# Quarter passes for the third column group of the experts, with a branch at its transposes

## The chip, the cores and the metric

The kernel runs on one core of a Trainium2 chip. A run's time is device microseconds from start to end; three runs of the kernel before took 1610.56, 1611.50 and 1614.88 us, a median of 1611.5. One more execution was profiled; its own time was 1617.83 us.

## The reference

The program is two layers of a transformer block on 256 tokens of width 1024. The second layer ends in a mixture of experts, and only that part is touched here:

```python
probs = jax.nn.softmax(logits, axis=-1)
top_p, top_i = lax.top_k(probs, TOP_K)              # 2 of 8 experts for a token
...
for e in range(N_EXPERTS):
    out = out + combine[..., e:e + 1] * _swiglu(h, w1[e], w3[e], w2[e])
# _swiglu: (silu(h @ w1) * (h @ w3)) @ w2, with w1, w3 of 1024 x 2816 and w2 of 2816 x 1024, fp32
```

The kernel gives each expert only the tokens that chose it. How many these are depends on the data: 64 on average, up to 128 in the part of the program that matters here (more than 128 would start a second pass, which these inputs don't need).

## The kernel before

**Weights.** The weights of an expert come as 35 blocks, each one DMA of 256 rows (two k-tiles of 128): 24 for W1 and W3 and 11 for W2. The 2816 inner columns are cut in three groups, two of 1024 columns and one of 768. For a group, four blocks of W1 follow each other and then four of W3 (`for g in range(3)`, L1665 on); after the groups come the 11 blocks of W2 with 1024 columns each. A block is 1 MB, or 768 KB in the third group. All DMAs are issued by SyncE (L97) in this order into 16 buffers, each as soon as a buffer is given back by the block that last used it.

**Tokens as the stationary operand.** In `passes` (L1613) the tokens of an expert are the weights of TensorE's array and the expert's weights stream through. For the first 64 tokens ("kind 0") the array is used as two halves of 64 columns: two matmuls side by side, one for the lower and one for the upper half of the group's inner columns, so that a bank of PSUM holds tokens by inner columns twice (`tiles`, L1615 to L1619). What happens for tokens beyond 64 is decided at run time by the count `num[e]` (`more`, L1597):

- up to 64 tokens: nothing more;
- up to 96: in the first two groups and in W2 the remaining 32 tokens ("kind 2") take four matmuls of 32 columns side by side, each over a quarter of the block's columns (`quart`, m = 32); in the third group they take the path of the next line;
- over 96: 64 more tokens ("kind 1") in two halves, like the first ones, into the second bank (`half`).

Branches are real ones: TensorE's sequencer compares and jumps (L1602 for 64, L1606 for 96). The other engines run the same instructions on either path.

**Between W3 and W2.** ScalarE takes silu of the W1 banks (L1687), VectorE multiplies by the W3 banks (L1689), and `transposes` (L1643) turns the product into W2's stationary operand: TensorE transposes of 128 columns (L1650), four for a group of 1024 and three for the third, for each of the two banks, and a copy to SBUF. `hidden` (L1656) finds the 64 or 32 tokens that belong to a k-tile in it. In the third group a quarter layout had no counterpart there, since 768 columns in quarters are 192, one and a half tiles; so `quarters` was passed as `g < 2`.

**Order.** A scheduler puts the instructions of every engine in a fixed order; an If with its bodies stays in one piece. In the first expert blocks of the next expert's W1 stand between the late W2 blocks. An expert's number in this text is its place in the order of work: the first is expert 0 of the model, the fourth the one with the most tokens.

Of the kernel before, what the change touches and what calls it, by code (L numbers as in the profile page):

```python
# [8 lines left out]
F32 = mybir.dt.float32  # L9
# [17 lines left out]
CAP = 128  # L27
# [155 lines left out]
HALF = 64  # L183
QUART = 32
# [25 lines left out]
def _body(ctx, tc, nc, I, out):  # L210
    V, A, PE, G, SP = nc.vector, nc.scalar, nc.tensor, nc.gpsimd, nc.sync
# [10 lines left out]
    def ps_x():  # L222
        return psx.tile([128, 512], F32, name="px", tag="px")
# [7 lines left out]
    def ctile(shape, dt=F32, name=None, pool=None):  # L231
        cnt[0] += 1
        name = f"{name}{cnt[0]}"
        return (mconst if pool else const).tile(shape, dt, name=name, tag=name)
# [11 lines left out]
    ident = ctile([128, 128], name="ident")  # L246
# [297 lines left out]
    cur = {}  # L544
# [854 lines left out]
    def moe_route():  # L1399

        Sp, M = pools["s"], pools["m"]
# [65 lines left out]
        def places(out, src):  # L1467
            for b in range(2):
                V.tensor_tensor(out=tmp[:, b], in0=src[:, b].unsqueeze(1).to_broadcast(sq), in1=ord_, op=OP.mult)
            V.tensor_reduce(out=out, in_=tmp, axis=AX.X, op=OP.add)  # L1470
# [4 lines left out]
        quart = M.tile([128, NE], F32, name="qu", tag="qu")  # L1475

        def tail():

            V.tensor_copy(out=fl[:, 2], in_=pos[:, 16:16 + NE])
            V.tensor_copy(out=fl[:, 3], in_=iota[:, 0:NE])  # L1480
            places(rt[:, 0:1, 12:14].rearrange("p o a e -> p (o a) e"), fl[:, 2:4])
            V.tensor_copy(out=cm[:, 1:].rearrange("p (a e) -> p a e", a=2), in_=rt[0:1, 0, 12:14])
            V.tensor_reduce(out=fl[:, 0, 0:1], in_=fl[:, 2], axis=AX.X, op=OP.max)
            V.tensor_copy(out=cm[:, 0:1], in_=fl[0:1, 0, 0:1])
            V.tensor_scalar(out=quart, in0=rt[:, 0, 12], scalar1=float(HALF + QUART), scalar2=None, op0=OP.is_le)
            V.tensor_tensor(out=rt[:, :, 3, 2:3], in0=rt[:, :, 4, 0:1], in1=rt[:, :, 4, 1:2], op=OP.add)
            V.reciprocal(out=rt[:, :, 3, 3:4], in_=rt[:, :, 3, 2:3])
            V.tensor_tensor(out=rt[:, :, 6, 0:2], in0=rt[:, :, 4, 0:2],
                            in1=rt[:, :, 3, 3:4].to_broadcast([128, 2, 2]), op=OP.mult)
            for i in range(2):  # L1490
                V.tensor_tensor(out=t(7 + i), in0=t(7 + i), in1=col(6, i), op=OP.mult)
            V.tensor_tensor(out=t(14), in0=t(7), in1=t(8), op=OP.add)
            places(t(10), t(14))

        cur["moe"] = dict(r=r, rt=rt, cm=cm, key=key, quart=quart, tail=tail)

    def moe_pass(stream, off, raw_pool, finish):
# [6 lines left out]
        M = lambda: pools["m"]  # L1504
# [3 lines left out]
        def block(W, j, c0, n, k0):  # L1508

            def src():  # L1510
                if j == 0:
                    w = W[0:1]
                else:
                    if j not in ids:
                        ids[j] = nc.values_load(cur["moe"]["cm"][0:1, 1 + NE + j:2 + NE + j],
                                                engines=[mybir.EngineType.SP], min_val=0, max_val=NE - 1)
                    w = W[bass.ds(ids[j], 1)]
                return w[:, k0 * 128:k0 * 128 + 256, c0:c0 + n].rearrange("o (k p) c -> p (o k) c", p=128)
            return stream.raw(src, 2, n, raw_pool)
# [5 lines left out]
        hp = []  # L1525
# [67 lines left out]
        def run_pend():  # L1593
            while pend:
                pend.pop(0)()

        def more(e, half, quart, none=lambda: None):  # L1597

            if off:
                half()  # L1600
                return
            with tc.If(num[e] > HALF) as c:  # L1602
                if quart is None:
                    half()
                else:
                    with tc.If(num[e] > HALF + QUART) as c2:  # L1606
                        half()
                    with c2.Else():
                        quart()
            with c.Else():  # L1610
                none()

        def passes(e, banks, w, n, lhs, first, last, quarters):  # L1613

            def tiles(bank, kind, k, m):  # L1615
                c = n // (128 // m)
                for q in range(128 // m):
                    PE.matmul(out=bank[m * q:m * q + m, 0:c], lhsT=lhs(kind, k), rhs=w[:, k, c * q:c * q + c],  # L1618
                              start=first and k == 0, stop=last and k == 1)  # L1619

            def rest():
                tiles(banks[0], 0, 1, HALF)

            def half():
                for k in range(2):
                    tiles(banks[1], 1, k, HALF)
                rest()

            def quart():
                for k in range(2):  # L1630
                    tiles(banks[1], 2, k, QUART)
                rest()

            tiles(banks[0], 0, 0, HALF)
            more(e, half, quart if quarters else None, rest)

        def expert(e):
            gt = {}
            gT = {}
            y = []  # L1640
            tabs = {}

            def transposes(g):  # L1643
                nb = 4 if g < 2 else 3
                gT[g] = M().tile([128, 2, nb, CAP], F32, name="gt", tag="gt" if g < 2 else "gt2")
                for i in range(2):
                    p = ps_x()
                    pv = p.rearrange("p (c s) -> p c s", c=4)[:, 0:nb]
                    for c in range(nb):
                        PE.transpose(out=pv[:, c], in_=gt[g][:, i, c * 128:c * 128 + 128], identity=ident)  # L1650
                    if i == 0:
                        A.activation(out=gT[g][:, i], in_=pv, func=AF.Copy)  # L1652
                    else:
                        V.tensor_copy(out=gT[g][:, i], in_=pv)

            def hidden(kk, kind):  # L1656

                g, d = min(kk // 8, 2), kk - 8 * min(kk // 8, 2)
                nb = 4 if g < 2 else 3
                if kind == 2 and g < 2:  # L1660
                    return gT[g][:, 1, d % 2, QUART * (d // 2):QUART * (d // 2) + QUART]
                c = HALF * (d // nb)
                return gT[g][:, min(kind, 1), d % nb, c:c + (HALF if kind < 2 else QUART)]

            for g in range(3):  # L1665
                n = 1024 if g < 2 else 768
                for wi, W in enumerate((W1, W3)):
                    for i in range(4):
                        raw = block(W, e, g * 1024, n, 2 * i)

                        def fn(hi, lo, g=g, n=n, wi=wi, i=i):
                            def lhs(kind, k):
                                c = (0, HALF, HALF)[kind]
                                return xg[e][:, 2 * i + k, c:c + (HALF, HALF, QUART)[kind]]

                            passes(e, hp[wi], hi[0], n, lhs, i == 0, i == 3, g < 2)
                            if wi == 0 and i == 1:
                                run_pend()
                                if g > 0:
                                    transposes(g - 1)  # L1680
                            if i == 3:
                                if wi == 0:
                                    gt[g] = M().tile([128, 2, 512], F32, name="esg", tag="s")
                                for b in range(2):
                                    c = slice(0, n // 2)
                                    if wi == 0:
                                        A.activation(out=gt[g][:, b, c], in_=hp[0][b][:, c], func=AF.Silu)  # L1687
                                    else:
                                        V.tensor_tensor(out=gt[g][:, b, c], in0=gt[g][:, b, c], in1=hp[1][b][:, c],  # L1689
                                                        op=OP.mult)  # L1690
                        stream.unit([sub(raw, lambda t: t, "raw")], fn)
            for ch in range(11):
                raw = block(W2, e, 0, 1024, ch * 2)

                def fn(hi, lo, ch=ch):
                    if ch == 0:
                        y.extend((ps_x(), hp[1][1]))
                    passes(e, y, hi[0], 1024, lambda kind, k: hidden(2 * ch + k, kind), ch == 0, ch == 10, True)
                    if ch == 1:
                        tabs["t"] = scatter_table(e)  # L1700
                    if ch == 2:
# [130 lines left out]
    start = res[0]  # L1832
# [32 lines left out]
    n = nc.values_load(cur["moe"]["cm"][0:1, 0:1], min_val=0, max_val=T)  # L1865
    with tc.If(n > CAP):
        rest = Stream(nc, wpool, WB)
        rest.open(["a"], [rawa], 2048, [RA])
        start = moe_pass(rest, CAP, "a", moe_finish)
# [27 lines left out]
```

## Time and profile before

| | |
|---|---|
| three runs | 1610.56, 1611.50, 1614.88 us (median 1611.5) |
| profiled execution | 1617.83 us, span 1616.1 us |
| PE (matmuls) busy | 1530.3 us, 95% of the span |
| DVE, ACT, POOL busy | 771.8, 577.9, 46.3 us |
| read from HBM | 455.58 MB, 283 GB/s over the span |
| weight blocks of the experts | 216 issues of 1024 KB and 64 of 768 KB |
| expert stage | from some 905 us to the end |
[...]

How to read it: PE and the DMA engines both look full over the expert stage, and the shares of the whole span say nothing of which of them ends last at a given place. The stage has to be cut into stretches. An fp32 matmul shows as two records of PE (and two weight loads, PEld), so record counts are twice the matmuls. The ends of matmul records are modelled and overlap the next ones; paces are read from the starts, as a stretch divided by the blocks in it.

### The profile page before, as it was taken

Reading aid. Unit: us, or ns where it says so; the run is one execution under the profiler, and the core shown is the slowest. Engines: PE = TensorE matmul, PEld = TensorE weight load, DVE = VectorE, ACT = ScalarE, POOL = GpSimd, SP = SyncE. Lnnn points to the kernel's source line nnn. Section 1 sums busy time; section 2 is a strip of 40 time slices with the busy share of each in tenths; the row PEclk is TensorE's granted clock in tenths of the full one; section 3 lists DMA queues with packets and bytes.
Section 4 is the critical chain, followed back from the end, with each engine's and each line's share of the span. In section 5 each row is a group of like instructions: output and inputs, shape, how many; then the busy total and the mean of one; then the engine's idle time right before and its main releaser. Section 6 shows DMA issues by size and latency. Waiting matters only on the chain. (4 is left out here: it accounts for less than half of the span.)

```text
span 1616.1 us, 26236 instructions
## 1 busy us (share of the span) xinstructions
PE 1530.3 (95%) x10586; PEld 1071.7 (66%) x10586; DVE 771.8 (48%) x1274; ACT 577.9 (36%) x924; POOL 46.3 (3%) x68
## 2 busy tenths in 40 slices
PE   3999999999989999999999899999899999999996
PEld 2999899989988999999999333343334333333332
DVE  7899687776776659976575310111101111110121
ACT  3676656655444477775764100011000010100010
POOL 2001010000000000002000000000000000000000
PEclk9999999999999999999998899999999999999998
DMA  9656677435688743554448599999999899999995
GB/s 363 234 184 205 242 249 282 161 127 193 240 280 310 263 149 117 184 196 157 157 157 331 185 351 334 393 407 404 408 405 397 277 380 407 404 407 405 408 404 212
DMA packets 162780, 459.29 MB, mean 284 GB/s; under 512 B 11454, under 2 KB 19716, under 8 KB 162600
## 3 DMA queue, kind: packets, MB, share of 16 engines
q1 hardware_dynamic: 162408, 456.55, 76.5%
q8 instruction: 140, 2.29, 0.6%
q14 instruction: 40, 0.33, 0.1%
q0 software_dynamic: 192, 0.11, 0.0%
HBM read 455.58 MB, written 1.05 MB: 283 GB/s over the span
## 5 line engine op out<-in xcount | busy, mean ns | idle before, releaser
L1618 PE MATMUL pm<-rawa,xg 128*64 128x512 f32 (+2 forms) x2368 | 412.8, 519 | 6.6 <-DMA rawa<-in_moe_w 2.9
L122 DVE TENSOR_TENSOR wl<-rawa,wh 128x1024 fp32r<-128x1024 f32 (+1 forms) x243 | 293.8, 1215 | 99.5 <-ACT wh L120 98.5
L120 ACT ACTIVATE wh<-rawa 128x1024 fp32r<-128x1024 f32 (+1 forms) x243 | 254.8, 1054 | 230.4 <-PE pm L578 107.7
L1618 PEld LDWEIGHTS pm<-rawa,xg 128*64 128x64 f32 (+1 forms) x2368 | 141.7, 130 | 259.7 <-issue 241.6
L577 PE MATMUL pm<-hh,wh 128*128 128x256 f32 x992 | 286.5, 289 | 5.6 <-ACT hh L552 4.6
L579 PE MATMUL pm<-hh,wl 128*128 128x256 f32 x992 | 284.2, 287 | 4.0 <-DVE wl L122 4.0
L578 PE MATMUL pm<-hl,wh 128*128 128x256 f32 x992 | 284.6, 287 | 1.6 <-DVE hl L553 0.8
L577 PEld LDWEIGHTS pm<-hh,wh 128*128 128x128 f32 x992 | 190.1, 192 | 9.1 <-ACT hh L552 4.8
L579 PEld LDWEIGHTS pm<-hh,wl 128*128 128x128 f32 x992 | 189.8, 191 | 5.3 <-DVE wl L122 5.0
L578 PEld LDWEIGHTS pm<-hl,wh 128*128 128x128 f32 x992 | 189.8, 191 | 2.9 <-DVE hl L558 1.2
L1618 PE MATMUL px<-rawa,gt 128*64 128x512 f32 x704 | 167.0, 599 | 5.6 <-DMA rawa<-in_moe_w 4.9
L1689 DVE TENSOR_TENSOR esg<-esg,pm 128x512 f32<-128x512 f32 (+1 forms) x48 | 29.5, 641 | 281.5 <-PE pm L1618 281.2
L591 PE MATMUL pm<-wl,hh 128*128 128x256 f32 x448 | 128.7, 287 | 1.6 <-DVE wl L122 1.6
L590 PE MATMUL pm<-wh,hh 128*128 128x256 f32 x448 | 128.8, 288 | 0.0
L592 PE MATMUL pm<-wh,hl 128*128 128x256 f32 x448 | 127.8, 285 | 0.0
L1618 PEld LDWEIGHTS px<-rawa,gt 128*64 128x64 f32 x704 | 46.9, 136 | 98.3 <-issue 88.9
L414 DVE SCALAR_TENSOR_TENSOR macc<-rawm,csil,macc 128x1024 f32<-128x1024 f32 x74 | 94.6, 1278 | 35.0 <-DMA rawm<-in_w_mod 34.6
L591 PEld LDWEIGHTS pm<-wl,hh 128*128 128x128 f32 x448 | 84.9, 189 | 2.0 <-DVE wl L122 1.8
L592 PEld LDWEIGHTS pm<-wh,hl 128*128 128x128 f32 x448 | 84.9, 189 | 0.2 <-issue 0.2
L590 PEld LDWEIGHTS pm<-wh,hh 128*128 128x128 f32 x448 | 84.9, 190 | 0.0
L1716 DVE COPY ys<-pm 128x512 f32<-128x512 f32 x8 | 5.5, 692 | 161.4 <-PE pm L1618 83.9
L1652 ACT ACTIVATE gt<-px 128x512 f32<-128x512 f32 (+1 forms) x24 | 13.5, 564 | 181.6 <-PE px L1650 181.6
(401 smaller groups left out, 1960.7 us busy)
## 6 DMA issues: line engine op xcount, KB each, us to landing
rawa<-in_moe_w SPq DMA_DIRECT2D x216, 1024.0 KB, 17.6
rawa<-in_w_in SPq DMA_DIRECT2D x68, 1024.0 KB, 6.2
rawa<-in_moe_w SPq DMA_DIRECT2D x64, 768.0 KB, 15.0
rawm<-in_w_mod SPq DMA_DIRECT2D x80, 512.0 KB, 8.3
rawa<-in_ffn_w SPq DMA_DIRECT2D x29, 1024.0 KB, 7.4
rawa<-in_w_branch SPq DMA_DIRECT2D x12, 1024.0 KB, 5.7
rawa<-in_w_out SPq DMA_DIRECT2D x8, 1024.0 KB, 5.5
rawa<-in_w_mod SPq DMA_DIRECT2D x7, 1024.0 KB, 10.1
```

The lines of the kernel that those rows point to most:

```text
L120: nc.scalar.activation(out=hv, in_=src, func=AF.Copy)
L122: nc.vector.tensor_sub(out=lv, in0=src, in1=hv.bitcast(F32))
L414: V.scalar_tensor_tensor(out=st["acc"], in0=src[:, 0], scalar=csil[:, k:k + 1], in1=st["acc"], op0=OP.mult, op1=OP.add)
L577: PE.matmul(out=o, lhsT=wh, rhs=xh[:, k], start=(k == 0), stop=False)
L578: PE.matmul(out=o, lhsT=wh, rhs=xl[:, k], start=False, stop=False)
L579: PE.matmul(out=o, lhsT=wl, rhs=xh[:, k], start=False, stop=(k == nk - 1))
L590: PE.matmul(out=o, lhsT=xh[:, k, c], rhs=wh, start=(k == 0), stop=False)
L591: PE.matmul(out=o, lhsT=xh[:, k, c], rhs=wl, start=False, stop=False)
L592: PE.matmul(out=o, lhsT=xl[:, k, c], rhs=wh, start=False, stop=(k == nk - 1))
L1618: PE.matmul(out=bank[m * q:m * q + m, 0:c], lhsT=lhs(kind, k), rhs=w[:, k, c * q:c * q + c], start=first and k == 0, stop=last and k == 1)
L1652: A.activation(out=gT[g][:, i], in_=pv, func=AF.Copy)
L1689: V.tensor_tensor(out=gt[g][:, b, c], in0=gt[g][:, b, c], in1=hp[1][b][:, c], op=OP.mult)
```

## The change

The third group gets the quarter path too: for 65 to 96 tokens the 32 tokens beyond 64 take four matmuls of 32 columns over 192 inner columns each, and the product is transposed in another layout: two transposes of 128 columns at offsets 0 and 64, and two matmuls of 64 columns that put columns 128 to 191 and 0 to 63 into the third tile, the second by way of `turn`, an identity rotated by 32 that POOL copies once. This layout is chosen by a branch at the transposes of the third group's second bank. In every block the second k-tile of the first 64 tokens now stands ahead of the matmuls for the tokens beyond 64 instead of behind them (the parameter `odd` is always False).

```diff
@@ moe_route, tail
+            turn = M.tile([128, CAP], F32, name="turn", tag="otmp")
+            G.tensor_copy(out=turn[:, 0:CAP - QUART], in_=ident[:, QUART:CAP])
+            G.tensor_copy(out=turn[:, CAP - QUART:CAP], in_=ident[:, 0:QUART])
+            cur["moe"]["turn"] = turn
@@ passes
-            def rest():
-                tiles(banks[0], 0, 1, HALF)
+            def rest(ks):
+                for k in ks:
+                    tiles(banks[0], 0, k, HALF)
             def half():
                 for k in range(2):
                     tiles(banks[1], 1, k, HALF)
-                rest()
             def quart():
                 for k in range(2):
                     tiles(banks[1], 2, k, QUART)
-                rest()
-            tiles(banks[0], 0, 0, HALF)
-            more(e, half, quart if quarters else None, rest)
...
+                rest((0,))
+                more(e, lambda: (rest((1,)), half()), lambda: (rest((1,)), quart()), lambda: rest((1,)))
@@ transposes
+                    def odd():
+                        for c in range(2):
+                            PE.transpose(out=pv[:, c], in_=src[:, c * 64:c * 64 + 128], identity=ident)
+                        PE.matmul(out=pv[0:64, 2], lhsT=src[:, 128:192], rhs=ident, start=True, stop=True)
+                        PE.matmul(out=pv[64:128, 2], lhsT=src[:, 0:64], rhs=cur["moe"]["turn"], start=True, stop=True)
+                    if i == 1 and g == 2 and not off:
+                        more(e, blocks, odd, blocks)
+                    else:
+                        blocks()
@@ hidden
-                if kind == 2 and g < 2:
-                    return gT[g][:, 1, d % 2, QUART * (d // 2):QUART * (d // 2) + QUART]
...
+                c, q = (d % 2, d // 2) if g < 2 else ((0, 0), (2, 0), (1, 1), (0, 2), (2, 2), (1, 3))[d]
+                return gT[g][:, 1, c, QUART * q:QUART * q + QUART]
@@ expert
-                            passes(e, hp[wi], hi[0], n, lhs, i == 0, i == 3, g < 2)
+                            passes(e, hp[wi], hi[0], n, lhs, i == 0, i == 3, False)
```

The order of PE's instructions in a block of the third group, here the first one of the first expert. `64x384` is a matmul of 64 columns with 384 streamed columns, `x2` two of them; all bodies of a branch are listed, the one for over 96 tokens first. Before (L1618 matmuls, L1602 the comparison with 64):

```order
L1618 MATMUL pm<-rawa,xg 64x384 x2
L1602 COMPARE_AND_BRANCH
L1618 MATMUL pm<-rawa,xg 64x384 x6
L1602 UNCONDITIONAL_BRANCH
L1618 MATMUL pm<-rawa,xg 64x384 x2
L1602 UNCONDITIONAL_BRANCH
```

After (L1623 matmuls, L1606 the comparison with 64, L1610 the one with 96):

```order
L1623 MATMUL pm<-rawa,xg 64x384 x2
L1606 COMPARE_AND_BRANCH
L1610 COMPARE_AND_BRANCH
L1623 MATMUL pm<-rawa,xg 64x384 x6
L1610 UNCONDITIONAL_BRANCH
L1623 MATMUL pm<-rawa,xg 64x384 x2
L1623 MATMUL pm<-rawa,xg 32x192 x8
L1610 UNCONDITIONAL_BRANCH
L1623 MATMUL pm<-rawa,xg 64x384 x2
L1606 UNCONDITIONAL_BRANCH
```

A body of eight matmuls of 32 columns and 192 streamed columns has come in, behind the two that finish the first 64 tokens, and a second comparison. With up to 64 tokens the same four matmuls run as before.

PE's order around the first W2 block of the first expert (`gt` is W2's stationary operand, `esg` the product that the transposes read; L1650, then L1660 and L1665 to L1667, are the transposes). Before:

```order
L1602 COMPARE_AND_BRANCH
L1606 COMPARE_AND_BRANCH
L1618 MATMUL pm<-rawa,gt 64x512 x4
L1618 MATMUL px<-rawa,gt 64x512 x2
L1606 UNCONDITIONAL_BRANCH
L1618 MATMUL pm<-rawa,gt 32x256 x8
L1618 MATMUL px<-rawa,gt 64x512 x2
L1606 UNCONDITIONAL_BRANCH
L1618 MATMUL px<-rawa,gt 64x512 x2
L1602 UNCONDITIONAL_BRANCH
L1650 MATMUL px<-ident_83,esg 128x128 x6
```

After, without the bodies of the W2 block's branch:

```order
L1660 MATMUL px<-ident_83,esg 128x128 x3
L1606 COMPARE_AND_BRANCH
...
L1606 COMPARE_AND_BRANCH
L1610 COMPARE_AND_BRANCH
L1660 MATMUL px<-ident_83,esg 128x128 x3
L1610 UNCONDITIONAL_BRANCH
L1665 MATMUL px<-ident_83,esg 128x128 x2
L1666 MATMUL px<-ident_83,esg 64x128
L1667 MATMUL px<-turn,esg 64x128
L1610 UNCONDITIONAL_BRANCH
L1660 MATMUL px<-ident_83,esg 128x128 x3
L1606 UNCONDITIONAL_BRANCH
```

The three transposes of the first bank have moved ahead of the W2 block's branch; those of the second bank stay behind it and are now the three bodies of a branch of their own.

## Rows read from the trace of the kernel before

**Rows 1.** Busy time of each engine in stretches of the expert stage (heading first).

```profile
core 0: us, PE busy (x) PEld busy (x) DVE busy (x) ACT busy (x) POOL busy (x), PEclk, DMA share, GB/s
954.30:979.00 24.70, 24.70 (x148) 10.71 (x144) 4.25 (x12) 2.45 (x5) 0.00 (x0) 1.00 0.96 340
979.00:1018.00 39.00, 38.92 (x301) 12.87 (x302) 1.56 (x4) 0.49 (x1) 0.00 (x0) 1.00 0.93 345
1018.00:1140.00 122.00, 120.36 (x602) 47.82 (x600) 24.80 (x52) 14.33 (x28) 0.00 (x0) 1.00 1.02 402
1140.00:1160.00 20.00, 16.24 (x72) 4.46 (x70) 0.69 (x1) 0.60 (x1) 0.00 (x0) 1.00 1.02 408
1160.00:1245.00 85.00, 84.56 (x432) 33.47 (x434) 10.60 (x21) 5.82 (x11) 0.00 (x0) 1.00 1.03 407
1245.00:1300.00 55.00, 55.00 (x250) 20.65 (x248) 6.62 (x13) 3.94 (x7) 0.00 (x0) 1.00 0.84 287
1300.00:1385.00 85.00, 83.08 (x406) 29.25 (x402) 14.16 (x27) 7.77 (x15) 0.00 (x0) 1.00 1.02 403
1385.00:1400.00 15.00, 11.49 (x66) 4.31 (x64) 1.76 (x4) 1.47 (x3) 0.00 (x0) 1.00 1.03 403
1400.00:1590.00 190.00, 188.81 (x1228) 70.85 (x1230) 29.65 (x54) 16.03 (x31) 0.00 (x0) 1.00 1.03 406
```

**Rows 2.** What the SyncE queue waited for, 954 to 1018 us: us, times, longest.

```profile
SPq L97 <- PE px L1618: 26.4, 11, 4.0
SPq L97 <- PE pm L1618: 18.5, 8, 2.9
```

**Rows 3.** Timeline at the last weight block: start, us, what, idle before.

```profile
1599.41 1.94 PE L1618 MATMUL px<-rawa,gt 128*64 128x512 f32 x8 [0.57 <-DMA rawa<-in_moe_w]
```

**Rows 4.** Groups by shape on PE, 880 us to end: count, busy, mean ns.

```profile
L1618 PE MATMUL pm<-rawa,xg 128*64 128x384 f32 x704 | 120.6, 489 | 2.3 <-DMA rawa<-in_moe_w 2.3
L1618 PE MATMUL pm<-rawa,xg 128*32 128x256 f32 x512 | 34.3, 385 | 0.0
```

**Rows 5.** Groups by shape, 915 to 1016 us (first expert).

```profile
L1618 PE MATMUL pm<-rawa,xg 128*64 128x384 f32 x128 | 22.5, 490 | 0.0
L1618 PE MATMUL pm<-rawa,xg 128*32 128x256 f32 x208 | 13.9, 385 | 0.0
L1650 PE MATMUL px<-ident,esg 128*128 128x128 f32 x22 | 3.3, 283 | 0.0
L1689 DVE TENSOR_TENSOR esg<-esg,pm 128x384 f32<-128x384 f32 x2 | 1.1, 555 | 6.2 <-PE pm L1618 6.1
```

**Rows 6.** Groups by shape on PE, 1430 to 1534 us (seventh expert).

```profile
L1618 PE MATMUL pm<-rawa,xg 128*64 128x384 f32 x128 | 21.3, 488 | 0.0
L1618 PE MATMUL pm<-rawa,xg 128*32 128x256 f32 x256 | 17.1, 385 | 0.0
```

**Rows 7.** Stretches of whole blocks, columns as in rows 1.

```profile
935.22:946.68 11.46, 11.46 (x98) 3.61 (x96) 0.00 (x0) 0.00 (x0) 0.00 (x0) 1.00 0.93 335
971.05:978.83 7.78, 7.78 (x49) 3.36 (x48) 1.52 (x5) 1.85 (x4) 0.00 (x0) 1.00 0.96 325
1171.73:1185.44 13.71, 13.71 (x66) 5.52 (x64) 0.54 (x1) 0.60 (x1) 0.00 (x0) 1.00 1.02 407
```

**Rows 8.** Timeline of the weight loads of one quarter block's narrow passes.

```profile
935.22 0.59 PEld L1618 LDWEIGHTS pm<-rawa,xg 128*32 128x32 f32 x16 [0.81 <-issue]
```

**Rows 9.** Page, section 3: instruction DMAs, packets, MB, share.

```profile
q8 instruction: 140, 2.29, 0.6%
```

**Rows 10.** The first comparison's line: ns min/median/max, first and last start.

```profile
L1602 PEldq COMPARE_BRANCH  x312: 65/208/4868, 902.9 to 1602.1; - x156
```

**Rows 11.** Waits from 880 us on: us, times, longest.

```profile
PE pm L1618 <- issue: 2.8, 6, 1.0
```

More of the change, by code (lines that the diff above doesn't have):

```diff
@@ L1611, in more, with passes @@
                 none()
-        def passes(e, banks, w, n, lhs, first, last, quarters):
+        def passes(e, banks, w, n, lhs, first, last, odd):
             def tiles(bank, kind, k, m):
@@ L1631, in quart @@
                     tiles(banks[1], 2, k, QUART)
-                rest()
-            tiles(banks[0], 0, 0, HALF)
-            more(e, half, quart if quarters else None, rest)
+            if odd:
+                more(e, lambda: (half(), rest((0, 1))), lambda: (quart(), rest((0, 1))), lambda: rest((0, 1)))
+            else:
+                rest((0,))
+                more(e, lambda: (rest((1,)), half()), lambda: (rest((1,)), quart()), lambda: rest((1,)))
         def expert(e):
@@ L1648, in transposes, with blocks @@
                     pv = p.rearrange("p (c s) -> p c s", c=4)[:, 0:nb]
-                    for c in range(nb):
-                        PE.transpose(out=pv[:, c], in_=gt[g][:, i, c * 128:c * 128 + 128], identity=ident)
+                    src = gt[g][:, i]
+                    def blocks():
+                        for c in range(nb):
+                            PE.transpose(out=pv[:, c], in_=src[:, c * 128:c * 128 + 128], identity=ident)
+                    def odd():
[5 more added lines that the diff above has]
+                        more(e, blocks, odd, blocks)
+                    else:
+                        blocks()
                     if i == 0:
@@ L1659, in hidden @@
                 nb = 4 if g < 2 else 3
-                if kind == 2 and g < 2:
-                    return gT[g][:, 1, d % 2, QUART * (d // 2):QUART * (d // 2) + QUART]
-                c = HALF * (d // nb)
-                return gT[g][:, min(kind, 1), d % nb, c:c + (HALF if kind < 2 else QUART)]
+                if kind < 2:
+                    c = HALF * (d // nb)
+                    return gT[g][:, kind, d % nb, c:c + HALF]
+                c, q = (d % 2, d // 2) if g < 2 else ((0, 0), (2, 0), (1, 1), (0, 2), (2, 2), (1, 3))[d]
+                return gT[g][:, 1, c, QUART * q:QUART * q + QUART]
             for g in range(3):
@@ L1697, in fn @@
                         y.extend((ps_x(), hp[1][1]))
-                    passes(e, y, hi[0], 1024, lambda kind, k: hidden(2 * ch + k, kind), ch == 0, ch == 10, True)
+                    passes(e, y, hi[0], 1024, lambda kind, k: hidden(2 * ch + k, kind), ch == 0, ch == 10, False)
                     if ch == 1:
```

## The prediction

> **What bounds the kernel now.** I read the expert stage alone (905 to 1616 us), since the change touches nothing ahead of it but two copies. First the busy time by stretch, for who has no room: PE or the DMA engines. The reader is to see two limits that take turns [rows 1]. The most that the DMA engines move is about 408 GB/s, and PE is busy nearly throughout, so neither alone tells which of them ends last. In the first expert (its third group and W2, 954 to 1018) PE has next to no idle time and the DMA engines move 340 to 345 GB/s. There the SyncE queue, which issues the weight loads, spends 44.9 of the 64 us from 954 to 1018 waiting for PE to give a buffer back [rows 2]: PE is the limit, and it hands its pace on to the DMA engines. From 1018 to 1140 they run at 402, and at 1140 to 1160 PE is idle 3.8 us (20.00 less 16.24): the limit has become the DMA. From 1245 to 1300, in the large fourth expert, PE has no idle time and the DMA engines fall to 287 GB/s: PE again. From 1300 to 1590 it is 403 to 406 GB/s, PE is idle 3.5 us at 1385 to 1400, and the last block's matmuls begin after a gap of 0.57 us that ends with the landing of their weights [rows 3]: DMA to the end.
>
> Then the shapes, for which experts the edit reaches. Each fp32 matmul leaves two records. A block of the third group gives 8 records of 64 columns x 384 for the first 64 tokens and 8 more for the second half; 8 experts of 8 blocks make 512, and the 704 there leave 192, three experts with over 64 tokens [rows 4]. The 32-wide form has 512 records in the first two groups, 256 an expert: two experts take the quarter path. One is the first expert and the other the seventh, at 1430 to 1534 [rows 5, 6]. The fourth takes the half path and runs the same matmuls as before.
>
> **The change part by part.** *A block of the third group.* Three stretches give the paces at full clock [rows 7]. Fourth expert: 13.71 us hold four half blocks (64 records and two tails), 3.43 each, which is 8 passes (two matmuls of 64 columns side by side) of 0.43 us for 512 columns. First expert, third group: 7.78 us hold three half blocks, 2.59 each, 8 passes of 0.324 for 384 columns. So a pass goes by its columns. Quarter block of the first groups: 11.46 us hold four, 2.87 each. Its four wide passes take 1.72 and its four narrow ones (four matmuls of 32 columns side by side, 256 long) half of that, 0.86, by columns: 2.58. The other 0.29 is what two changes of width cost, 64 to 32 and back. The third group has none of them now, since it uses 64 columns alone; the change brings two to every block. A new block: four wide passes of 0.324 make 1.29, four narrow ones of 192 columns 0.65 at 0.162, two changes 0.29: 2.23 us. Against 2.59 that is 0.36 a block, 2.9 us in an expert.
>
> The unmeasured term is the 192-column pass. By columns it is 0.162; if something in the narrow form sets its pace it stays at the 0.216 of 256 columns, the block is 2.44 and the expert saves 1.2 us. It can't beat its columns, unless the change of width shrinks as well; with that at nothing an expert saves 5.2. I take 0.162: 16 narrow weight loads start within 0.59 us [rows 8], 37 ns each, and a pass has four, 0.148.
>
> [...]
>
> *Order inside a block.* The second k of the first 64 tokens now stands before the narrow passes, inside the branch. The number of width changes stays at two. Bank 0 is ready earlier, bank 1 later; at the end of the third group the first transposes stand before the branch of the first W2 block and wait for VectorE's product on bank 0, which now runs beside the narrow passes. Nothing, while they cover it; if they don't, one product of 384 columns, 0.56 us (1.1 for two), once an expert [rows 5].
>
> *The transposes.* Three become two wide ones and two of 64 columns side by side. 22 records take 3.3 us [rows 5], 0.30 a transpose, so the matmuls cost between 0 and 0.30 more, and there are two more changes of width, 0.29. I take 0.3 in the first expert. The other experts run the same three behind two more jumps.
>
> *The two copies on POOL.* POOL is at 0.00 in every stretch [rows 1] and PE needs them 70 us later: nothing.
>
> *More instructions.* PE's program grows from 9021 to 9331 rows, 3.4%. Of 2.29 MB of instructions for all engines [rows 9] that is at most 0.08 MB, 0.2 us at 408 GB/s.
>
> *Where the two gains go.* First expert: 2.9 − 0.3 = 2.6 us on PE. Its buffers come back sooner, one each 2.23 us, while a 1 MB load takes 2.57 at 408 GB/s; so 8 x 0.34 = 2.7 us of loads are put off into 979 to 1018, where the engines have 39.0 x (1 − 345/408) = 6.0 us to spare. From there all moves up by 2.6: the DMA-bound stretch, the PE-bound fourth expert, the DMA-bound rest. Seventh expert: it stands in the last DMA-bound stretch. PE comes earlier to the last weights, and waits. In the profile that leaves nothing. The profiled execution took 1617.8 (a span of 1616.1 and 1.7 around it) and the median run 1611.5, 6.3 less; if a part of this is faster loads, PE and DMA end closer together than the 0.57 us shows, and some of the gain survives. I put it between 0 and 2.6 and take 0.6.
>
> Sum: −2.6 − 0.6 + 0.2 = −3.0 us, 1617.8 to 1614.8 in a profile, and on the median 1608.5.
>
> **The rivals.** *Both experts pay.* If outside the profile the tail is bound by PE, the second 2.6 counts: −5.2 + 0.2, 1606.5; with cheaper changes of width some 1605. For it: the 6.3 us between profile and runs, and PE at 188.8 of 190 us busy before 1590. Against it: the gap of 0.57 that ends with a DMA, and 3.5 us of idle PE just ahead of the seventh expert.
>
> *The narrow pass keeps its pace.* 1.2 − 0.3 in the first expert, with 0.2 for code: 1610.8, no change. For it: the shorter the pass, the more any fixed part weighs, and 0.148 of loads stand close to 0.162.
>
> *Slower: jumps get exposed.* In the PE-bound first and fourth expert all 16 third-group blocks now hold a second compare and longer bodies to jump over. A compare has a median of 208 ns, and PE lost 2.8 us in 6 gaps without a releaser, 0.47 each [rows 10, 11]. One such gap a block makes 7.5 us: −3.0 + 7.5, 1616.0, and with any in the transposes or the DMA-bound experts beyond. It decides from 0.19 us a block on. Against it: the quarter blocks of the first two groups carry the same compares and jumps, and their 2.87 is all accounted for above; the fourth expert's blocks carry them too and run at 3.43, 8 passes of 0.43.
>
> [...]
>
> **How the numbers follow.** First expert alone, with a part of the seventh: 0.46. Both: 0.22. No shorter pass: 0.18. Jumps: 0.11. Anything else: 0.03. A measurement of this kernel tells 0.3%, 4.8 us, from no change, so faster begins at 1606.7. Nearly all of "both" and a little of the likeliest lie there: 0.24. Slower needs 1616.3: about 0.11. Within: 0.65. The range goes from "both" with cheaper changes of width, 1604, to the pace kept plus what runs differ by upward (1614.9 against 1611.5), 1613.5.
>
> **What would show it.** In the profile after, the 64 x 384 form has 576 records and a 32 x 192 form 256. The third group of the first expert takes 2.9 us less than its 24.7, with narrow passes 0.162 apart; passes 0.216 apart show the second rival, gaps ahead of the first matmul behind a jump the third. The DMA engines reach 400 GB/s about 2.6 us earlier, before 1018, and PE waits some 3 us for the last weights in place of 0.57. If that wait has not grown while PE has less to do, the seventh expert pays as well and my reading of the tail is wrong. If the first expert's third group is shorter and the stretch at 1140 to 1160 begins no earlier, the hand-over from PE to DMA is wrong.

## The result and the profile after

The changed kernel took 1626.15 us (median of six runs, 1621.58 to 1626.76) and the kernel before, on the same chip, 1612.37 (six runs, 1609.61 to 1617.81). The ratio is 1.0081, its 95% interval 1.0063 to 1.0098: slower by 0.8%, 13.8 us between the medians. The prediction was 1608.5, with 1604.0 to 1613.5 as its range. Its sign is wrong.

The narrow passes came as predicted. Three blocks of the first expert's third group after, columns as in [rows 1] (to be read against the second line of [rows 7]):

```profile
968.27:974.96 6.69, 6.69 (x73) 2.71 (x72) 1.17 (x4) 1.74 (x4) 0.00 (x0) 1.00 0.97 328
```

6.69 us for three are 2.23 a block, the predicted figure, against 2.59 in [rows 7]. The shapes of the seventh expert after, 1435 to 1537 us, columns as in [rows 6]:

```profile
L1623 PE MATMUL pm<-rawa,xg 128*64 128x384 f32 x64 | 12.1, 499 | 0.0
L1623 PE MATMUL pm<-rawa,xg 128*32 128x192 f32 x128 | 6.9, 332 | 0.0
```

Half of the 384-column records are gone and 128 narrow ones are there, in this expert and in the first. So the time was lost elsewhere. In the changed kernel TensorE's products stand at line 1623 and its transposes at 1660 to 1667. The waits of TensorE in the expert stage after, 895 to 1620 us (us in total, times, longest):

```profile
PE pm L1623 <- issue: 18.1, 17, 2.0
PE px L1748 <- ACT ys L1738: 1.4, 2, 0.7
PE px L1623 <- issue: 1.2, 1, 1.2
...
PE px L1660 <- DVE esg L1712: 0.7, 1, 0.7
```

And in the kernel before, the lines beside [rows 11]:

```profile
PE px L1618 <- DMA rawa<-in_moe_w: 4.9, 6, 1.8
PE pm L1618 <- DMA rawa<-in_moe_w: 2.9, 5, 0.9
```

"Issue" is time in which nothing that the profile shows held the engine back. It went from 2.8 us in 6 gaps [rows 11] to 18.1 in 17 (3.6 of it in two gaps of the first expert that have another cause, below), while the 7.8 us of waits for weights vanished: TensorE is now so late that every weight block is there before it is wanted. The stretches after show the same, columns as in [rows 1]:

```profile
954.30:979.00 24.70, 23.95 (x237) 10.18 (x235) 4.37 (x12) 2.83 (x6) 0.00 (x0) 1.00 0.99 358
979.00:1018.00 39.00, 38.28 (x282) 12.18 (x278) 1.25 (x2) 1.57 (x3) 0.00 (x0) 1.00 0.91 327
1018.00:1140.00 122.00, 114.73 (x555) 46.00 (x555) 21.99 (x42) 11.49 (x22) 0.00 (x0) 1.00 1.03 405
...
1400.00:1590.00 190.00, 182.36 (x1272) 67.39 (x1270) 29.72 (x54) 14.54 (x28) 0.00 (x0) 1.00 1.03 406
```

From 1018 to 1140 TensorE is now idle 7.3 us (1.6 in [rows 1]) and from 1400 to 1590 7.6 us (1.2). Where, a timeline of PE in the third expert (at most 64 tokens, a *plain* one from here on) tells: start, us, what, and in brackets the idle time before.

```profile
1113.53 5.37 PE L1623 MATMUL pm<-rawa,xg 128*64 128x512 f32 x24 [0.85 <-issue]
1119.39 4.09 PE L1623 MATMUL pm<-rawa,xg 128*64 128x512 f32 x20 [0.48 <-issue]
...
1125.24 0.87 PE L1623 MATMUL pm<-rawa,xg 128*64 128x384 f32 x4 [0.60 <-issue]
...
1131.00 4.09 PE L1623 MATMUL pm<-rawa,xg 128*64 128x384 f32 x24 [0.72 <-issue]
1136.76 0.87 PE L1623 MATMUL pm<-rawa,xg 128*64 128x384 f32 x4 [1.67 <-issue]
```

The gaps stand 5.76 to 5.86 us apart, whatever the shape. From 1131.00 to 1136.76 three blocks are run (24 records, 8 a block); they need 4.09 us, and then the engine stands for 1.67. The DMA queues tell what comes at that pace. Section 3 of the profile after (against [rows 9]):

```profile
q8 instruction: 152, 2.49, 0.6%
```

And the same queue in the 34 us from 1108 to 1142 alone:

```profile
q8 instruction: 6, 0.10, 1.2%
```

I take a packet of this queue for a piece of the program, an *instruction page* (a page from here on): 2.49 MB / 152 = 16.4 KB. Six in 34 us are one every 5.7 us. Three of the packets start at 1122.72, 1128.47 and 1134.22 us, and the gaps above end 2.5 us after each, at 1125.24, 1131.00 and 1136.76. So, as I read it, the engine gets a page, runs three blocks from it, and waits for the next.

### The profile page after: what moved, and what is told of

It is laid out like the page before. It is cut to its first block, busy times and chain, and to the rows that moved or that the text cites. A ratio compares the mean times of both kernels' runs of the same rounds, so it can differ in the third digit from the quotient of the medians.

```text
span 1624.0 us, 26544 instructions
## 1 busy us (share of the span) xinstructions
PE 1534.5 (94%) x10720; PEld 1078.2 (66%) x10720; DVE 772.0 (48%) x1274; ACT 577.9 (36%) x924; POOL 47.7 (3%) x70
## 3 DMA queue, kind: packets, MB, share of 16 engines
q8 instruction: 152, 2.49, 0.6%
## 5 line engine op out<-in xcount | busy, mean ns | idle before, releaser
L1623 PE MATMUL pm<-rawa,xg 128*64 128x512 f32 (+3 forms) x2496 | 409.2, 503 | 18.7 <-issue 18.1
L1623 PEld LDWEIGHTS pm<-rawa,xg 128*64 128x64 f32 (+1 forms) x2496 | 140.1, 128 | 271.2 <-issue 256.8
L1623 PE MATMUL px<-rawa,gt 128*64 128x512 f32 x704 | 167.2, 598 | 1.2 <-issue 1.2
L1623 PEld LDWEIGHTS px<-rawa,gt 128*64 128x64 f32 x704 | 50.1, 136 | 88.4 <-issue 84.1
L1710 ACT ACTIVATE esg<-pm 128x512 f32<-128x512 f32 (+1 forms) x48 | 24.3, 559 | 155.5 <-PE pm L1623 155.5
```

## What the experiments were to tell apart

Three theories. *Code*: the third group now writes out 20 products a block in the program (2 ahead of the branch, 6, 10 and 2 in its bodies) where it had 10 (2, 6, 2), a product being one matmul of the program, two records in the trace; a plain expert runs 4 of them in 1.3 us, but the pages hold all, and they arrive no faster. *Jumps*: it is the compares and jumps, not what is jumped over. *Order*: it is the second pair of products that now stands ahead of the passes for the tokens beyond 64.

**The third group's bodies alone, never run.** The kernel before, with a body of quarter passes in the third group behind a count that doesn't occur (where `off` is set it stays as before):

```diff
-            more(e, half, quart if quarters else None, rest)
+            if quarters or off:
+                more(e, half, quart, rest)
+            else:
+                with tc.If(num[e] > HALF) as c:
+                    with tc.If(num[e] > 250) as c2:
+                        quart()
+                    with c2.Else():
+                        half()
+                with c.Else():
+                    rest()
```

> The kernel before, with a body in each third-group block that is never entered: for over 64 tokens a second comparison, with 250, chooses between a quarter body (eight matmuls of 32x192 and the two of the first 64 tokens) and the half body that before ran alone. No count reaches 250, so what runs is what ran before, plus one comparison a block in the three experts over 64 tokens; 640 matmuls more lie in PE's program. Code theory (the bodies that are jumped over are fetched with the rest, a 16 KB page takes some 5.8 us while the weight loads fill the DMA engines, and experts of up to 64 tokens run through a page sooner): slower than before by 10 to 17 us, gaps without a releaser ahead of the third group's matmuls in the plain experts, 9 to 12 more instruction packets. Jump theory (each comparison and jump in the PE-bound experts is exposed): also slower, 8 to 15 us, but with gaps in the first and fourth expert. Order theory (the loss comes from the new order inside a block and at the transposes): no change.

Measured: 1618.37 us, ratio 1.0040 (1.0018 to 1.0061), 7 us slower without one product more to run. Its waits of PE, 895 to 1620 us:

```profile
PE pm L1618 <- issue: 13.7, 15, 1.8
PE px L1618 <- issue: 2.6, 4, 1.6
```

Its program has 151 pages (2.47 MB) where the kernel before has 140 [rows 9], and but for the first expert's the gaps stand in the plain experts, as in the changed kernel. TensorE's products in the expert stage come in exactly the order of the kernel before. The loss is below the range that I gave the code theory (10 to 17 us), so code can't be all of the 13.8.

**The same compare and jumps with a short body.** As above, with `rest()` in place of `quart()`: 12 products a block.

> The same with a short body that is never entered: only the two matmuls of the first 64 tokens. The comparisons and jumps are those of x1_dead, the code grows by 128 matmuls in place of 640. Code theory: a fifth of the loss of x1_dead, 0 to 4 us slower than before. Jump theory: the same loss as x1_dead within 3 us. Order theory: no change.

Measured: 1614.76 us, 1.0021 (1.0008 to 1.0034), 143 pages. Its largest wait for issue, 895 to 1620 us:

```profile
PE pm L1618 <- issue: 2.0, 4, 1.0
```

The order of TensorE's products is again that of the kernel before, and as many compares and jumps run as in the run above. The jump theory wanted that run's time within 3 us; it is 3.6 us faster, with intervals that overlap, so it is the gaps that decide, and they are there only with the longer body. The 512 products between the two programs are 8 pages, 64 to a page. The 3.5 us by which this run still is slower than the kernel before I can't place: none of its traced waits has grown by more than 0.2 us, and its expert stage, from the start of the first product to the start of the last, is no longer than that of the kernel before (694.5 us against 695.6; 702.1 in the run above).

**The order alone.** The kernel before with `rest()` ahead of the passes in `half` and `quart`, nothing else.

> The kernel before with the new order inside a block alone: the second k-tile of the first 64 tokens stands at the head of the branch's bodies, the matmuls for the tokens beyond 64 behind it. Third group on the half path, transposes and amount of code as before. Order theory: slower by 8 to 14 us. Code and jump theory: slower by 1 to 4 us, from the loads of the counts in the first expert, whose two gaps grew from 0.58 and 1.03 us to 1.58 and 2.05, and from the wait for VectorE at the first transposes.

Measured: 1617.28 us, 1.0039 (1.0021 to 1.0057). More than the code theory allowed, less than the order theory wanted. Its first two waits for issue are in the first expert, 895 to 925 us, where PE loads the counts (three and four register loads between blocks). The same two waits there in this run, in the changed kernel, and in the kernel before:

```profile
PE pm L1618 <- issue: 3.6, 2, 2.0
```
```profile
PE pm L1623 <- issue: 3.6, 2, 2.0
```
```profile
PE pm L1618 <- issue: 1.6, 2, 1.0
```

The loads begin while the last products ahead of them are still in the array. In the old order the last ones are a pair of 512 columns, and in the kernel before the first loads start 1.7 and 1.8 us ahead of the end of these products; in the new order they are narrow passes, and in the changed kernel it is 0.7 and 0.8 us. So the cover is a microsecond shorter, twice. With the wait of the first transposes for VectorE (0.7) and one more for ScalarE's `ys` (0.7), which these two kernels share, the order costs 3.4 us that can be pointed at; the expert stage is 3.3 us longer than in the kernel before (698.9 against 695.6). The rest of the 6.1 us between the medians is not placed.

**Four products ahead of the branch, an empty body.** The changed kernel with both pairs first:

```diff
-                rest((0,))
-                more(e, lambda: (rest((1,)), half()), lambda: (rest((1,)), quart()), lambda: rest((1,)))
+                rest((0, 1))
+                more(e, half, quart)
```

> The changed kernel with shorter code: both k-tiles of the first 64 tokens stand once ahead of the branch, and its bodies hold only the matmuls for the tokens beyond 64 (none for up to 64). What runs is the same, in the same order. PE's program has 424 matmuls less than before, 1120 less than the changed kernel. Code theory: the gaps without a releaser in the plain experts go, the first and seventh experts keep their third group of some 22 and 19 us: 3 to 10 us faster than before, some 1605. Jump theory: as slow as the changed kernel, 1622 to 1628, since the jumps are the same. Order theory: 1622 to 1628 as well, since the order is the same.

Measured: 1676.17 us, 1.0396 (1.0371 to 1.0421). A miss by 70 us, by something that I had not thought of. All gaps for issue went; others came. Its waits, 895 to 1680 us:

```profile
PE pm L1623 <- PEq L1606: 11.3, 48, 0.8
PE px L1660 <- DVE esg L1712: 6.0, 7, 0.9
PE px L1623 <- PEq L1606: 5.4, 27, 0.4
```

PEq is the sequencer. One of its records on the line of the branch, columns as in [rows 10]:

```profile
L1606 PEldq EVENT_SEMAPHORE  x180: 51/51/51, 1006.2 to 1664.7; - x180
```

The changed kernel has 5 of these on the same line; with a body without a product in every block there are 180. In the records the instruction starts some 40 ns behind the modelled end of the last product, so the array drains 180 times. The plain blocks take 2.09 us in place of 1.72; 180 x 0.37 is 67 us, an estimate, against 65 us above the kernel before.

**The old order, all the code.** The changed kernel with the passes beyond 64 first:

```diff
-                more(e, lambda: (rest((1,)), half()), lambda: (rest((1,)), quart()), lambda: rest((1,)))
+                more(e, lambda: (half(), rest((1,))), lambda: (quart(), rest((1,))), lambda: rest((1,)))
```

> The changed kernel, but inside a block the passes for the tokens beyond 64 again come before the second pair of products of the first 64, in every body, as in the kernel before. The number of products in the program is that of the changed kernel (20 a block in all three groups). Code theory (the third group's bodies fill the instruction pages with products that are jumped over): nothing returns, 1621 to 1626 us, issue gaps of 14 to 18 us stay in the experts with at most 64 tokens. Order theory (the changed order costs what it cost alone, 6.1 us): 1616 to 1620 us, with the issue gaps as they are in the plain experts and the time returned in the first, fourth and seventh experts. Were the order the whole of it: 1608 to 1610 us.

Measured: 1623.27 us, 1.0060 (1.0038 to 1.0081), inside the code theory's range and above the order theory's. 0.0021 of the ratio came back, 3.4 us, which is also what the traced waits had for the order (the intervals overlap, so it is the trace that carries this, not the time). 152 pages, and the gaps stay:

```profile
PE pm L1623 <- issue: 14.7, 15, 1.8
PE px L1623 <- issue: 4.5, 5, 1.7
```

**Three products ahead of the branch.** The same, with one product of the second pair moved ahead and one left in each body, 18 a block; and the kernel before with the same.

```diff
                 rest((0,))
+                tiles(banks[0], 0, 1, HALF, 0, 1)
...
+                more(e, lambda: (half(), last_one()), lambda: (quart(), last_one()), last_one)
```

> The changed kernel with the order of the kernel before and a shorter branch: three of the four products of a block's first 64 tokens stand ahead of the branch, and each of its three bodies holds only the fourth, so that no body is empty; 18 products a block in the program instead of 20. At 64 products to an instruction page and 1.72 us a block of a plain expert, a page is then used up in 6.1 us instead of 5.5, which is longer than the 5.7 to 5.9 us at which pages followed one another. Code theory: the issue gaps of the plain experts go to under 5 us, 1604 to 1611 us. Order theory without the code: as the run with the old order alone, 1608 to 1620 us, no different from it within 2 us. Jump theory (each jump costs, whatever is jumped over): no gain over the run with the old order alone, 1616 us or more.

> The kernel before with the shorter branch alone: three of the four products of the first 64 tokens ahead of the branch, one in each body; 18 products a block in the first two groups and in the second weight, 9 in the third group, instead of 20 and 10. Code theory: its issue gaps (2.8 us in 6) go, the waits for weights take some of it, 1608 to 1612 us, the same as before within 3 us. Jump theory: no difference, 1611 to 1613. Order of the products: the last 64-column product now follows the passes of the tokens beyond 64 alone, 1610 to 1616.

Measured: 1630.66 (1.0138, 1.0094 to 1.0182) and 1636.20 (1.0138, 1.0117 to 1.0160). One execution of 1651.83 us lifts the first ratio; by the medians it is 1.0108. Both expectations of the time missed, and the first part held: the gaps for issue are gone (1.3 us in one, and none). What came is seen in the waits of the first of the two:

```profile
PE px L1665 <- DVE esg L1717: 10.6, 12, 1.5
PE px L1753 <- ACT ys L1743: 5.7, 8, 0.7
...
PE px L1623 <- issue: 1.3, 1, 1.3
```

The scheduler now stands the transposes and the scatter elsewhere between the blocks, in all experts, where TensorE waits 16.3 us for their operands (0.7 and 1.4 in the changed kernel). The two kernels thus changed more than the length of the code; the rest of what they lost I have not followed up.

**Half of the weight bytes.** The changed kernel and the kernel before, each loading only the first 128 rows of a block and using them for both halves; the instructions of a block are the same:

```diff
-                return w[:, k0 * 128:k0 * 128 + 256, c0:c0 + n].rearrange("o (k p) c -> p (o k) c", p=128)
-            return stream.raw(src, 2, n, raw_pool)
+                return w[:, k0 * 128:k0 * 128 + 128, c0:c0 + n].rearrange("o (k p) c -> p (o k) c", p=128)
+            return stream.raw(src, 1, n, raw_pool)
...
-                    PE.matmul(out=bank[m * q:m * q + m, 0:c], lhsT=lhs(kind, k), rhs=w[:, k, c * q:c * q + c],
+                    PE.matmul(out=bank[m * q:m * q + m, 0:c], lhsT=lhs(kind, k), rhs=w[:, 0, c * q:c * q + c],
```

> The changed kernel with half of the experts' weight bytes: of each block only the first 128 rows are loaded, and both halves of the block are multiplied with these; products, branches and program are as they were. If pages of instructions come late because they share the DMA engines with the weights: pages follow one another at 3 to 4 us, the issue gaps (18.1 us) go to under 4 us and the time is 1600 to 1609 us. If a page takes its 5.7 us, or the jumps cost, whatever else the DMA engines do: the gaps stay at 15 to 20 us, 1618 to 1626 us.

> The kernel before with half of the experts' weight bytes in the same way. Page theory: the issue gaps (2.8 us) and the waits for weights (7.8 us in the expert stage) go, 1602 to 1608 us, and the changed kernel with half the bytes is 1 to 4 us faster than this one, as the blind sum had it. If the gaps don't come from the load of the DMA engines: 1603 to 1608 here, and the changed kernel with half the bytes 12 to 18 us slower than it.

Measured: 1623.21 and 1599.68 us. The waits of the first (895 to 1620 us):

```profile
PE px L1748 <- ACT ys L1738: 5.6, 8, 0.7
PE pm L1623 <- issue: 3.7, 2, 2.1
```

The two gaps that are left are the count loads of the first expert. Those of the plain experts are gone, with all 152 pages still fetched. The DMA engines move 232 GB/s here from 1018 to 1140 us and 176 from 1400 to 1590, against 405 and 406 in the changed kernel. Read one by one, the packets of q8 from 1007 us on start less than 5.3 us apart in 27 of 87 cases (down to 3.1 while weights stream), against 4 of 87 in the changed kernel. And those 4 stand where the weights leave room in the changed kernel itself: one at the end of the stretch from 1245 to 1300 us, where the DMA engines move 261 GB/s, and three after 1605 us, when the loads have all but ended (49 GB/s from 1600 to 1616). So by these runs a page is late because the weights occupy the DMA engines. The comparison of the times fell through, and both lie outside what was expected: with weights expected sooner, the scheduler set a different order in both kernels (blocks of the next expert between the products of W2, the scatter ahead of a block), and 23.5 us lie between them without gaps for issue. What of it is which, these runs don't say.

**One common tail.** The changed kernel with the second pair once behind the inner branch and once in the body for at most 64 tokens; 18 products a block, no fewer jumps, no empty body; and the kernel before with the same.

```diff
-        def more(e, half, quart, none=lambda: None):
+        def more(e, half, quart, none=lambda: None, tail=lambda: None):
...
                     with c2.Else():
                         quart()
+                    tail()
             with c.Else():
                 none()
...
-                more(e, lambda: (rest((1,)), half()), lambda: (rest((1,)), quart()), lambda: rest((1,)))
+                more(e, half, quart, lambda: rest((1,)), lambda: rest((1,)))
```

> The changed kernel with the second pair of the first 64 tokens' products written once behind the inner branch (one copy for both kinds of more than 64 tokens, one in the body for at most 64) instead of once in each of the three bodies: 18 products a block in the program instead of 20, no body empty, both products of a pair next to each other, the tokens beyond 64 first. The jumps that are run are the same in number. Code theory: the issue gaps of the plain experts (19 us with the old order) go to under 4 us as they did with three products ahead of the branch, the unpaired products of that run do not come, and the blind sum holds: 1604 to 1612 us. Jump theory: as many jumps, 1620 to 1626 us. Pairs alone (what slowed the two kernels with 18 products was not the pairs): 1625 to 1632 us.

> The kernel before with the same common tail: 18 products a block in the first two groups and W2, 10 in the third as before. Code theory: the issue gaps (2.8 us) go and the waits for weights (7.8 us) take up to all of it: 1607 to 1612 us. The changed kernel with the tail is 0 to 4 us faster than this one, by the narrow passes. Jump theory: as before, 1611 to 1613 us.

Measured: 1612.88 us (12 runs), ratio 1.0000 (0.9984 to 1.0016), and 1614.78, 1.0012 (0.9996 to 1.0028). Against the run with the old order and all the code, two products less in a block of the program took away all that was left of the loss. (TensorE's order is not wholly that run's: some transposes and blocks of the next expert stand elsewhere. The pair of runs with the same order is that of the bodies that never run.) Waits of the first, 895 to 1620 us:

```profile
PE px L1624 <- DMA rawa<-in_moe_w: 7.7, 11, 1.4
PE pm L1624 <- DMA rawa<-in_moe_w: 4.3, 9, 0.7
PE pm L1624 <- issue: 2.9, 4, 1.1
...
PE px L1624 <- issue: 1.1, 1, 1.1
```

Its pages are 143, and the plain third group runs through again; PE's timeline in the same expert as above:

```profile
1116.46 7.32 PE L1624 MATMUL pm<-rawa,xg 128*64 128x384 f32 x44
1123.97 0.87 PE L1624 MATMUL pm<-rawa,xg 128*64 128x384 f32 x4 [0.20 <-issue]
```

Six blocks with one gap of 0.20 us. The code theory gave 1604 to 1612 us and is missed by 0.9; the jump theory's 1620 to 1626 is far off, though 553 compares and jumps run on the two comparisons' lines in place of 518. For the kernel before the tail brought nothing: it is 2.8 us above what I gave at most, its issue gaps fell to 1.9 us, and its waits for weights rose from 7.8 to 12.1. The changed kernel with the tail is 1.9 us faster than this one, inside the 0 to 4 expected, with intervals that overlap.

**The tail ahead of the inner branch.** Meant to bring back the new order with the short code:

```diff
             with tc.If(num[e] > HALF) as c:
+                head()
                 if quart is None:
...
-                more(e, lambda: (rest((1,)), half()), lambda: (rest((1,)), quart()), lambda: rest((1,)))
+                more(e, half, quart, lambda: rest((1,)), lambda: rest((1,)))
```

> The changed kernel with the second pair of the first 64 tokens' products once ahead of the inner branch (in the body for more than 64 tokens) and once in the body for at most 64: 18 products a block, in the order of the changed kernel, where the passes of the tokens beyond 64 stand last in a block; it differs from the kernel with the common tail in that place alone. Code theory with the order as a second, smaller term: the waits at the two count loads of the first expert are 1.6 and 2.1 us as in the changed kernel (0.6 and 1.1 with the tail), the issue gaps of the plain experts stay under 4 us, and the time is 2 to 5 us above that with the tail, 1614 to 1618 us. If the order costs nothing once the code is short: 1611 to 1614 us. If the order is the larger term: 1619 us or more.

Measured: 1612.74 us (12 runs), 0.9994 (0.9979 to 1.0008). It tests nothing of the order: the scheduler took the inner If first and set the pair behind it, and TensorE's products run in the same sequence as with the common tail. It is a second measurement of that kernel, and the two agree. So the new order was never measured with the short code.

## Why the prediction was wrong

*The block of the third group: right.* 2.23 us predicted and measured; the 192-column pass goes by its columns. The rival "the narrow pass keeps its pace" falls.

*More instructions: the step that failed.* I put "at most 0.08 MB, 0.2 us". Both factors are wrong. The rows of the order that I scaled by fold repeated products into one row, so that eight new ones counted as one: the program grew by 12 pages, 0.20 MB, not by 0.08. And its price is not bytes over the rate of the DMA engines but the pace of single pages, one every 5.7 us while the weights stream. In the plain experts the kernel before lived on the third group: three of its blocks of 512 columns took 5.2 us of TensorE for 60 products in the program, by an estimate from the 64 products to a page 5.5 us for a page that takes 5.7 or more to come, and the third group with 10 products a block made up for it: in the third expert six of its blocks run through without a gap (48 records in 7.96 us from 1121.72). With 20 products there too, at 1.3 us a block, nothing does. Returning two products a block (the common tail against the old order with all the code) gave 0.0060 of the ratio, 9.7 us. The 11 pages more for bodies none of whose products runs (151 against 140) were fetched all the same, and in the changed kernel the waits for pages come to 15.7 us of gaps (19.3 ahead of products, less the 3.6 at the count loads).

*"Jumps get exposed": the right sign, the wrong mechanism and place.* I had gaps in the first and fourth experts, where bodies are run. They are in the plain ones, where no product of the new bodies is run, and with more jumps the common tail has 4.0 us of gaps in 5, among them the two count loads. My argument against, that the first two groups carry the same bodies without loss, was read off experts that run them: a quarter block lasts 2.87 us, and three of them 8.6, longer than a page takes. I never priced the same bodies in a plain block of 1.72 us.

*Order inside a block: nothing while covered, else 0.56 us a product.* Cover was missing at the place that I had named and at one that I had not: the first transposes wait 0.7 us, near the 0.56; the count loads lose 2.0 us more.

*Where the two gains go.* With the code undone, none is left that these runs can tell: 1612.88 against 1613.16. I let the first expert's 2.6 us pass through by loads that move up; they did not move up by that. Counted from the stage's first product, the same weight bytes land 1.6 us earlier than in the kernel before near the end of the first expert, 0.4 us earlier in the third, and no earlier behind the fourth. TensorE's waits for weights are 12.0 us in place of 7.8, as if the gain were handed on as a wait; but the kernel before with the tail has 12.1 without a narrow pass, so this is not shown. The interval ends at 0.9984, so of the 3.0 us forecast some 2.6 at most can be there.

*The sum.* By the ratios, code took 9.7 us, order 3.4, narrow passes and transposes nothing that can be told: 13.1, against 13.8 between the medians. These are steps of one chain of kernels, so that they add up by the way they are taken. The test of the sum is the two edits to the kernel before: the bodies alone took 7.2 us and the order alone 6.1, together 13.3. The traced expert stage has 695.6 us before and 707.1 changed, 6.5 more with the bodies alone, 3.3 more with the order alone and 1.1 more with the tail. So code is the larger term and order the smaller; their sizes are known to some 3 us. The 3.5 us of the run with a short body, and as much of the order's 6.1 as the stage doesn't show, no term here explains.

## What to carry to other kernels

- A body that a branch jumps over was fetched all the same here (151 pages against 140): count the products written out per microsecond of the shortest path, and compare that with the pace of instruction pages while the DMA engines are full (here 64 products in 5.7 us).
- Put what all paths share once, behind the inner branch; but leave a product in every body: here an empty one drained the array, 0.37 us a block.
- Where "issue" gaps stand at equal distances whatever the shape of the work (here 5.76 to 5.86 us), look for a fetch, not for a wait in the kernel.

## What the runs showed that I had not expected

A page of 16.4 KB took 5.7 us and more from one to the next while 405 GB/s of weights streamed, and down to 3.1 with half the bytes streaming. A body without a product cost 0.37 us a block. The register loads between two blocks of the first expert cost 0.6 and 1.0 us behind a pair of 512 columns, and 1.6 and 2.1 behind narrow passes.
